# A decoder layer on one core: whole-row loads of p, first products by halves of depth, other banks for the first stacks, y split in four portions

## The chip, the cores and the metric

The kernel runs on one core of a Trainium2 chip. The metric is the device time of one execution in microseconds (us): before the change the median of three runs is 2273.17 us (2273.09 to 2273.24). Engines: TensorE (PE; PEld is its weight load), VectorE (DVE), ScalarE (ACT), GpSimd (POOL) and SyncE (SP), whose queue issues the loads and stores. Each engine works its instructions in order.

## The reference

One hybrid decoder layer on 1024 tokens of width 1024, all in float32:

```python
x = x + 0.5 * swiglu(rms_norm(x, ffn1_norm), ffn1_w_gate, ffn1_w_up, ffn1_w_down)      # d_ff 2816
h = rms_norm(x, mix_norm)
fq, fk, fv, f_logit, sq, sk, sv, g_fox, g_sb = split_columns(h @ w_in)
y_fox = forgetting_attention(rms_norm(fq, q_norm), rms_norm(fk, k_norm), fv, log_sigmoid(f_logit + forget_bias))
y_sb = stick_breaking_attention(sq, sk, sv)                                            # 8 heads of 64 each
x = x + (sigmoid(g_fox) * (y_fox @ w_branch_fox) + sigmoid(g_sb) * (y_sb @ w_branch_sb)) @ w_out
x = x + 0.5 * swiglu(rms_norm(x, ffn2_norm), ffn2_w_gate, ffn2_w_up, ffn2_w_down)
x = x + sigmoid(rms_norm(x, ple_norm) @ w_ple_gate) * (p @ w_ple_proj)                 # p: 1024 x 256
```

## The kernel before

A product of float32 operands is made of three: each operand is split into a high part (rounded, a CAST on ACT, line 112 or 136) and a low part (the rest, a subtraction on DVE, line 113, or on POOL, line 146), and high x high, low x high and high x low are added in one PSUM bank. There are eight banks: three `sc`, two `pt`, one `av`, two `pf`; `ps2` goes round the `sc` and `av` banks, `ps1` round `pt` and `pf`. A bank is used again only when its readers are through.

**The start** (`first_entry`). x is not needed for the last term's product p @ w_ple_proj, so the kernel makes it first and stores it (`pd`). p comes transposed, 256 x 1024; p and its weights are each two blocks k of 128 rows and 1024 columns. Eight loads of half blocks (`load_p`: block k, columns half h) are issued by SP, six of them ahead of the tiles of x. `busy(10)` gives TensorE ten matmuls on zeros meanwhile. `project(t, d)` makes the product of token tile t and half d of the width: six matmuls (line 1208), three products by two blocks k. Between the 16 calls stand the norms of the first four x tiles: `norm_stat` (ACT, POOL), `norm_mul` (DVE), and the transposes `norm_high` (TensorE, line 219, then ACT) and `norm_low` (DVE). The first products of the feed-forward follow (`plain`, line 419) with transposes of the other four tiles in `combo_a`. In this part the order of each engine's work is as the code is written.

**Attention**. There a scheduler orders instructions by itself within the given dependencies. `forget_sums` is followed by a gate unit and the first stacks: `fox_stack_units` transposes normalized q and k (line 785) into a `pf` bank, and `fill_stacks` reads it with two ACT and two DVE instructions (lines 770 to 773). Units of projections (`nat_steps`, line 691, `feat_steps`, line 699), each in a `pf` bank, are interleaved as filling with 16 heads of four steps c: `scores` (lines 889, 890; reductions at 894, exp at 900, its scaling on POOL at 902; the stick-breaking scans at 865) and `apply` (transposes 941, their parts 943 on ACT and 944 on DVE, values 963).

**y**. From head 14 on, the finished outputs y of the attention come back from memory: `load_y` loads blocks of 128 rows, `split_y` splits each (one ACT and one DVE instruction of 128 x 1024). `Y_AT` says at which head and step: first what is split, then what is loaded. Blocks 4 to 6 go into the buffer of blocks 0 to 2.

Of the kernel before, what the change touches and what calls it, by code (L numbers as in the profile page):

```python
# [18 lines left out]
P = 128  # L19
S = 1024  # L20
D = 1024
# [17 lines left out]
def tile_hybrid_decoder_layer(  # L39
# [33 lines left out]
    def bank(tag):  # L73
        return pp.tile([P, 512], F32, tag=tag, bufs=PSUM[tag], name=nm("ps"))
# [5 lines left out]
    def ps2():  # L80
        ring[1] += 1
        return bank(("sc", "sc", "sc", "av")[ring[1] % 4])
# [4 lines left out]
    def pe(ins):  # L87
        order("pe", ins)
# [99 lines left out]
    def busy(n):  # L188

        if "zero" not in last:  # L190
            last["zero"] = slot("T", [P, 512], BF16)
            nc.vector.memset(last["zero"][:], 0.0)
        z, ps = last["zero"], bank("av")
        for _ in range(n):
            pe(nc.tensor.matmul(ps[:], z[:, 0:P], z[:], start=True, stop=True))
# [17 lines left out]
    def norm_mul(N, t):  # L213
        nc.vector.scalar_tensor_tensor(N["h"][t][:], N["x"][:, t, :], N["r"].pop(t)[:], N["g"][:], ALU.mult, ALU.mult)
# [559 lines left out]
        nc.sync.dma_start(f(KH[a, cs]), f(KH[b, cs]))  # L774
        nc.sync.dma_start(f(KL[a, cs]), f(KL[b, cs]))

    def fox_stack_units(cell, hh, out_cell):
        def unit(half):
            if half == 0:
                out_cell["st"] = new_stacks()  # L780
            cs = slice(half * 512, half * 512 + 512)
            N = cell["n"][half]
            ps = bank("pf")
            for q in range(4):
                pe(nc.tensor.transpose(ps[:, q * P:(q + 1) * P], N[:, q, hh].rearrange("p s d -> p (s d)"), identf[:]))
# [238 lines left out]
    def attention():  # L1024
# [160 lines left out]
    def first_entry(F):  # L1185

        def load_x(t):
            nc.sync.dma_start(X[t // 4][:, t % 4, :], x[0, t * P:(t + 1) * P, :])

        raw = {"p": [slot("T", [P, S]) for _ in range(2)], "w": [slot("Q", [P, D]) for _ in range(2)]}  # L1190
        src = {"p": kp(p), "w": kp(w_ple_proj[0])}
        op = {"p": slot("H", [P, 2, 2, S], F32R), "w": slot("H", [P, 2, 2, D], F32R)}
        outs = {}

        def load_p(a, k, h):
            cs = slice(h * 512, h * 512 + 512)
            nc.sync.dma_start(raw[a][k][:, cs], src[a][:, k, cs])

        def split_p(a, k, h, eng_lo):
            cs = slice(h * 512, h * 512 + 512)  # L1200
            split(op[a][:, 0, k, cs], op[a][:, 1, k, cs], raw[a][k][:, cs], nc.scalar, eng_lo)

        def project(t, d):
            ps = ps2()
            i = 0
            for a, b in ((0, 0), (1, 0), (0, 1)):
                for k in range(2):
                    pe(nc.tensor.matmul(ps[:], op["p"][:, a, k, t * P:(t + 1) * P], op["w"][:, b, k, d * 512:d * 512 + 512], start=(i == 0), stop=(i == 5)))  # L1208
                    i += 1
            if d == 0:  # L1210
                outs[t] = slot(("RAW", "RAW", "GF", "RN", "Q", "Q")[t % 6], [P, D])
                nc.scalar.copy(outs[t][:, 0:512], ps[:])
            else:
                nc.vector.tensor_copy(outs[t][:, 512:D], ps[:])
# [5 lines left out]
        def projects(t):  # L1220
            project(t, 0)
            project(t, 1)

        for h, a in ((0, "pw"), (1, "w")):
            for k in range(2):
                for c in a:
                    load_p(c, k, h)
# [10 lines left out]
        for k in range(2):  # L1238
# [6 lines left out]
        load_x(4)  # L1245
        store_p(0)
        norm_stat(N[0], 0, "PT", True)
        projects(1)
        norm_mul(N[0], 0)
        load_x(5)  # L1250
        store_p(1)
        norm_stat(N[0], 1, "WL", True)
        projects(2)
        norm_mul(N[0], 1)
        for k in range(2):
            split_p("p", k, 1, nc.gpsimd)
        load_x(6)
        store_p(2)
        norm_stat(N[0], 2, "WL", True)
        projects(3)  # L1260
        norm_mul(N[0], 2)
        load_x(7)
        store_p(3)
        norm_stat(N[0], 3, "PT", True)
        norm_high(N[0], 0, ps1)
        projects(4)
        norm_low(N[0], 0)
        norm_mul(N[0], 3)
        F["load"](1)
        store_p(4)  # L1270
        norm_high(N[0], 1, ps1)
        projects(5)
        norm_low(N[0], 1)
        store_p(5)
        norm_high(N[0], 2, ps1)
        F["prep"](0, 1)
        projects(6)
        norm_low(N[0], 2)
        store_p(6)
        norm_high(N[0], 3, ps1)  # L1280
        norm_stat(N[1], 0, "Y", True)
        projects(7)
        norm_low(N[0], 3)
        store_p(7)
        F["prep"](0, 2)
        norm_stat(N[1], 1, "Y", True)
        F["plain"](0, 0, (0,))
        norm_mul(N[1], 0)
        norm_stat(N[1], 2, "PT", True)
        norm_mul(N[1], 1)  # L1290
# [263 lines left out]
```

## Time and profile before

| | |
|---|---|
| median of three runs | 2273.17 us |
| profiled execution | 2273.31 us, its span 2271.6 us |
| TensorE busy | 2247.5 us |
| granted clock, mean | 0.997 |
| DVE, ACT, POOL busy | 1467.7, 975.5, 821.8 us |

The span runs from the first to the last instruction. In a timeline or wait row the bracket names how long the engine was idle before and what ended that. Rows by windows give busy time of PE, PEld, DVE, ACT and POOL, then the granted TensorE clock, the share of the DMA engines and GB/s. "DMA to landing" is the time from issue to the end of a transfer.

### The profile page before, as it was taken

How to read it: one execution, taken by the hardware profiler on the slowest of the kernel's cores; microseconds unless marked ns; L12 is line 12 of the kernel's file. 1: busy time of each engine (PE TensorE's matmuls, PEld its weight loads, DVE VectorE, ACT ScalarE, POOL GpSimd, SP SyncE). 2: the span in 40 equal slices, each digit the busy share in tenths (PEclk: the TensorE clock that was granted, in tenths of full speed). 3: DMA queues.
4: the chain of work that ended last, by engine and by line, in shares of the span. 5: the costliest groups of instructions: out<-in, count | busy, mean ns of one | idle time of the engine just before them, and what ended most of it. 6: DMA issues, size and time to landing. Idle time of an engine off the chain costs nothing.

```text
span 2271.6 us, 30620 instructions
## 1 busy us (share of the span) xinstructions
PE 2247.5 (99%) x11440; PEld 1911.8 (84%) x11440; DVE 1467.7 (65%) x2206; ACT 975.5 (43%) x1740; POOL 821.8 (36%) x756
## 2 busy tenths in 40 slices
PE   8999999999999999999999999999999999999999
PEld 6888888888889999998988888888888888888887
DVE  6955555487874566656666676889655555778752
ACT  6433333333343455555555564246333333434431
POOL 1144343410024546645556644410534343200111
PEclk9999999999999999999999999999999999999999
DMA  6223232474431222222124245832423232656132
GB/s 250 70 101 127 79 130 79 156 288 148 158 131 48 84 75 71 75 66 72 50 70 116 61 125 196 287 121 65 139 79 130 79 130 79 252 195 217 64 103 92
DMA packets 186949, 276.01 MB, mean 122 GB/s; under 512 B 27176, under 2 KB 109352, under 8 KB 186800
## 3 DMA queue, kind: packets, MB, share of 16 engines
q1 hardware_dynamic: 186800, 274.05, 36.2%
q8 instruction: 90, 1.47, 0.3%
q14 instruction: 59, 0.48, 0.1%
HBM read 190.35 MB, written 75.27 MB: 117 GB/s over the span
## 4 chain that ended last, share of the span: by engine, by line
PE 95%; DVE 3%; ACT 1%; issue 1%; DMA 0%; POOL 0%; SPq 0%; POOLq 0%; DVEq 0%; ACTq 0%
PE ps L464 35%; PE ps L359 21%; PE ps L699 11%; PE ps L691 8%; PE ps L1496 4%; PE ps L1159 4%; PE ps L963 3%; PE ps L941 3%; PE ps L890 1%; PE ps L889 1%; PE ps L419 1%; PE ps L1208 1%; PE ps L219 1%; DVE RN L865 1%; DVE H L113 0%
## 5 line engine op out<-in xcount | busy, mean ns | idle before, releaser
L359 PE MATMUL ps<-H,H 128*128 128x512 f32 x2184 | 497.7, 389 | 1.2 <-DVE X L367 1.2
L359 PEld LDWEIGHTS ps<-H,H 128*128 128x128 f32 x2184 | 409.3, 188 | 86.7 <-issue 2.0
L464 PE MATMUL ps<-H,WL 128*128 128x512 f32 x1008 | 239.4, 389 | 0.8 <-ACT WL L112 0.8
L464 PEld LDWEIGHTS ps<-H,WL 128*128 128x128 f32 x1008 | 189.1, 188 | 40.5 <-ACT WL L112 1.2
L699 PE MATMUL ps<-H,WH 128*128 128x512 f32 x768 | 210.4, 401 | 1.4 <-DVE PT L814 1.4
L699 PEld LDWEIGHTS ps<-H,WH 128*128 128x128 f32 x768 | 136.2, 188 | 24.4 <-DVE PT L814 2.1
L146 POOL TENSOR_TENSOR WL<-Y,WH 128x512 fp32r<-128x512 f32 (+1 forms) x10 | 14.4, 1467 | 382.6 <-ACT WH L136 382.6
L944 DVE TENSOR_TENSOR PT<-ps,PT 128x512 fp32r<-128x512 f32 (+1 forms) x160 | 101.1, 633 | 75.4 <-ACT PT L943 74.5
L146 POOL TENSOR_TENSOR WL<-RAW,WH 128x512 fp32r<-128x512 f32 (+1 forms) x104 | 124.1, 1214 | 61.0 <-ACT WH L136 47.8
L464 PE MATMUL ps<-H,Q 128*128 128x512 f32 x600 | 143.1, 389 | 0.0
L367 DVE SCALAR_TENSOR_TENSOR X<-ps,X 128x512 f32<-128x512 f32 x168 | 109.0, 687 | 50.9 <-PE ps L359 50.9
L691 PE MATMUL ps<-WH,H 128*128 128x256 f32 (+1 forms) x896 | 133.6, 288 | 3.7 <-DVE KL L773 2.1
L464 PEld LDWEIGHTS ps<-H,Q 128*128 128x128 f32 x600 | 112.6, 188 | 23.4
L943 ACT CAST PT<-ps 128x512 fp32r<-128x512 f32 (+1 forms) x160 | 87.4, 548 | 95.4 <-PE ps L941 94.0
L691 PEld LDWEIGHTS ps<-WH,H 128*128 128x128 f32 x896 | 117.8, 191 | 5.6 <-issue 2.3
L464 PE MATMUL ps<-X,WL 128*128 128x512 f32 x504 | 121.1, 389 | 0.0
L464 PEld LDWEIGHTS ps<-X,WL 128*128 128x128 f32 x504 | 94.6, 188 | 19.6
L699 PE MATMUL ps<-H,WL 128*128 128x512 f32 x384 | 108.5, 399 | 0.0
L963 PE MATMUL ps<-PT,X 128*128 128x256 f32 (+1 forms) x640 | 103.9, 282 | 3.9 <-DVE PT L944 3.9
L963 PEld LDWEIGHTS ps<-PT,X 128*128 128x128 f32 x640 | 94.2, 190 | 15.2 <-DVE PT L944 6.0
L902 POOL TENSOR_TENSOR T<-T,l 128x128 f32<-128x128 f32 (+3 forms) x64 | 73.3, 1149 | 93.0 <-DVE l L901 90.6
L260 POOL TENSOR_TENSOR PT<-GF,RN 128x512 f32<-128x512 f32 x20 | 33.2, 1658 | 186.0 <-DVE GF L507 101.8
(400 smaller groups left out, 4725.4 us busy)
## 6 DMA issues: line engine op xcount, KB each, us to landing
hidden<-PT SPq DMA_DIRECT2D x40, 512.0 KB, 3.0
WH<-in_ffn_w_gate_dram SPq DMA_DIRECT2D x38, 512.0 KB, 4.8
Q<-hidden SPq DMA_DIRECT2D x24, 512.0 KB, 6.6
hidden<-RN SPq DMA_DIRECT2D x22, 512.0 KB, 2.6
RAW<-in_w_in_dram SPq DMA_DIRECT2D x22, 512.0 KB, 4.4
KH<-in_ffn_w_up_dram SPq DMA_DIRECT2D x20, 512.0 KB, 6.2
KL<-in_ffn_w_up_dram SPq DMA_DIRECT2D x20, 512.0 KB, 6.9
T<-in_ffn_w_down_dram SPq DMA_DIRECT2D x20, 512.0 KB, 4.8
```

What stands on the lines that cost most here:

```text
L146: ins = eng_lo.tensor_sub(lo[part], raw[part], f(hi[part]))
L359: pe(nc.tensor.matmul(groups[g][t][:], act[:, a, k, t * P:(t + 1) * P], wt[:, b, k, :], start=(fresh and n == 0), stop=(i in (6, 1, 4) and ...
L367: nc.vector.scalar_tensor_tensor(xs, groups[g][t][:], scale, xs, ALU.mult, ALU.add)
L464: pe(nc.tensor.matmul(ps[:], hl[:, a, k, :], rhs(m, b, k), start=(first and i == 0), stop=(final and i == 11), skip_group_check=True))
L691: pe(nc.tensor.matmul(ps[:, :n], hT[t // 4][a][:, k, (t % 4) * P:(t % 4 + 1) * P], w[k // 4][b][:, k % 4, :n], start=(i == 0), stop=(i == ...
L699: pe(nc.tensor.matmul(ps[:], w[a][:, k, :], hT[half][b][:, k, :], start=(i == 0), stop=(i == 23)))
L902: nc.gpsimd.tensor_mul(T[:, :n], T[:, :n], l[:].broadcast_to([P, n]))
L943: high = nc.scalar.copy(pt[:, 0, :width], ps[:, :width])
L944: low = nc.vector.tensor_sub(pt[:, 1, :width], ps[:, :width], f(pt[:, 0, :width]))
L963: pe(nc.tensor.matmul(o, lh, r, start=(kpair == c and i == 0), stop=(kpair == 0 and i == 3)))
L1159: pe(nc.tensor.matmul(ps[:], w[a][:, k, :], yT[g][b][:, k, half * 512:half * 512 + 512], start=(i == 0), stop=(i == 11)))
L1496: pe(nc.tensor.matmul(ps, hT[t // 4][a][:, k, (t % 4) * P:(t % 4 + 1) * P], pl["w"][d, k // 2][b][:, k % 2, cs], start=(i == 0), stop=(i = ...
```

## The change

Three edits. (1) At the start p and its weights come in four loads of whole blocks; eleven dummy matmuls instead of ten; `project` takes several units and goes through the blocks k outermost, so that the first call works at four banks, all products of block 0 ahead of those of block 1; the eviction alternates between ACT and DVE by t + d; two x tiles are loaded ahead of the gain and all others behind, and norms, `prep` and `combo_a` are placed anew. (2) The first stacks (h = 0) use the `pt` banks. (3) The splits of y stand in four places instead of two.

```diff
-        def load_p(a, k, h):
-            cs = slice(h * 512, h * 512 + 512)
-            nc.sync.dma_start(raw[a][k][:, cs], src[a][:, k, cs])
+        def load_p(a, k):
+            nc.sync.dma_start(raw[a][k][:], src[a][:, k, :])
...
-        def project(t, d):
+        def project(units, ring):
+            banks = [ring() for _ in units]
             i = 0
-            for a, b in ((0, 0), (1, 0), (0, 1)):
-                for k in range(2):
+            for k in range(2):
+                for a, b in ((0, 0), (1, 0), (0, 1)):
+                    for ps, (t, d) in zip(banks, units):
+                        pe(nc.tensor.matmul(ps[:], op["p"][:, a, k, t * P:(t + 1) * P], op["w"][:, b, k, d * 512:d * 512 + 512], start=(i == 0), stop=(i == 5)))
                     i += 1
+            for ps, (t, d) in zip(banks, units):
+                if t not in outs:
+                    outs[t] = slot(("RAW", "RAW", "GF", "RN", "Q", "Q", "T", "T")[t], [P, D])
+                if (t + d) % 2:
+                    nc.vector.tensor_copy(outs[t][:, d * 512:d * 512 + 512], ps[:])
+                else:
+                    nc.scalar.copy(outs[t][:, d * 512:d * 512 + 512], ps[:])
...
+        for k in range(2):
+            for c in "pw":
+                load_p(c, k)
         nc.scalar.activation(stat([P, 1], "ss")[:], mhalf[:, 0:1], AF.Silu)
-        busy(10)
+        busy(11)
         for k in range(2):
             for c in "pw":
                 split_p(c, k, 0, nc.vector)
         load_x(0)
+        load_x(1)
         N.append(combo_begin(X[0], ffn1_norm[0]))
         N.append(combo_begin(X[1], None, N[0]))
-        for t in range(1, 4):
+        for t in range(2, NT):
             load_x(t)
-        for k in range(2):
-            load_p("p", k, 1)
         F["load"](0)
-        project(0, 0)
+        project([(t, 0) for t in range(4)], ps2)
         for k in range(2):
             split_p("w", k, 1, nc.vector)
-        project(0, 1)
...
         norm_stat(N[0], 0, "PT", True)
...
         for k in range(2):
             split_p("p", k, 1, nc.gpsimd)
+        norm_stat(N[0], 1, "WL", True)
+        project([(0, 1)], ps1)
+        norm_mul(N[0], 0)
+        project([(1, 1)], ps1)
...
+        norm_high(N[0], 0, ps1)
+        project([(4, 0)], ps2)
+        norm_low(N[0], 0)
+        norm_mul(N[0], 2)
+        project([(4, 1)], ps2)
...
         F["plain"](0, 0, (0,))
         norm_mul(N[1], 1)
+        norm_stat(N[1], 3, "PT", True)
         F["prep"](0, 5)
-        norm_stat(N[1], 3, "PT", True)
+        F["a"](0)
+        norm_mul(N[1], 2)
         F["plain"](0, 0, (1,), False)
-        norm_mul(N[1], 2)
-        F["a"](0)
+        F["a"](1)
         norm_mul(N[1], 3)
-        F["a"](1)
...
-            ps = bank("pf")
+            ps = bank(tag)
...
-            return fox_stack_units(qk[h // 2], h % 2, stacks[h])
+            return fox_stack_units(qk[h // 2], h % 2, stacks[h], "pt" if h == 0 else "pf")
...
-    Y_AT = {(14, 0): ((), range(4)), (14, 3): (range(4), (4, 5, 6)), (15, 1): ((4, 5, 6), ())}
+    Y_AT = {(14, 0): ((), range(4)), (14, 3): ((0, 1), ()), (15, 0): ((2, 3), (4, 5, 6)), (15, 1): ((4, 5), ()), (15, 2): ((6,), ())}
```

What it makes of the engines' rows is shown at three places (a number behind a name tells the buffers apart). First TensorE at the start, before and after, from the last dummy on; H_102 holds p, H_103 the weights:

```order
L195 MATMUL ps_114<-T_112 128x512
L1208 MATMUL ps_147<-H_103,H_102 128x512 x6
L1208 MATMUL ps_160<-H_103,H_102 128x512 x6
L1208 MATMUL ps_176<-H_103,H_102 128x512 x6
L1208 MATMUL ps_185<-H_103,H_102 128x512 x6
```

```order
L195 MATMUL ps_112<-T_110 128x512
L1208 MATMUL ps_148<-H_103,H_102 128x512
L1208 MATMUL ps_149<-H_103,H_102 128x512
L1208 MATMUL ps_150<-H_103,H_102 128x512
L1208 MATMUL ps_151<-H_103,H_102 128x512
```

Six matmuls in a row went to one bank; now they go round four banks, and that six times, before single banks follow. ACT at the same place, before and after, from the last of the first four casts:

```order
L112 CAST H_103<-Q_101 128x512
L1212 COPY RAW_154<-ps_147 128x512
L112 CAST H_103<-Q_100 128x512
L112 CAST H_103<-Q_101 128x512
L206 ACTIVATE PT_170,ss_171<-X_94 128x1024
```

```order
L112 CAST H_103<-Q_101 128x512
L1216 COPY RAW_176<-ps_148 128x512
L1216 COPY GF_180<-ps_150 128x512
L112 CAST H_103<-Q_100 128x512
L112 CAST H_103<-Q_101 128x512
L206 ACTIVATE PT_188,ss_189<-X_94 128x1024
```

Two copies out of banks now stand ahead of the casts of the weights' other halves.

Second, DVE behind the first stacks (T and l belong to the first step's score tiles), from the fill of the second half of the first stack, before and after:

```order
L772 SCALAR_TENSOR_TENSOR Q_5684<-ps_5726,gqk,Q_5684 64x512
L773 SCALAR_TENSOR_TENSOR KL_5686<-ps_5726,gqk,KH_5685 64x512
L901 RECIPROCAL l_5744<-l_5744 128x1
L772 SCALAR_TENSOR_TENSOR Q_5753<-ps_5756,gqk,Q_5753 64x512
L773 SCALAR_TENSOR_TENSOR KL_5755<-ps_5756,gqk,KH_5754 64x512
L894 ISA T_5808,m_5809<-GF_5737,ps_5812 128x128
```

```order
L772 SCALAR_TENSOR_TENSOR Q_5681<-ps_5723,gqk,Q_5681 64x512
L773 SCALAR_TENSOR_TENSOR KL_5683<-ps_5723,gqk,KH_5682 64x512
L901 RECIPROCAL l_5741<-l_5741 128x1
L894 ISA T_5805,m_5806<-GF_5734,ps_5809 128x128
L894 ISA m_5806 128x1
L772 SCALAR_TENSOR_TENSOR Q_5750<-ps_5753,gqk,Q_5750 64x512
L773 SCALAR_TENSOR_TENSOR KL_5752<-ps_5753,gqk,KH_5751 64x512
```

The first reduction of the second score tile (T_5808, now T_5805) has moved ahead of the fill of the next stack. Third, DVE at (14,3); H<-X are the splits of y, before and after:

```order
L865 SCALAR_TENSOR_TENSOR RN_12369<-GF_12368,RN_12369 128x384
L113 TENSOR_TENSOR H_12439<-X_12127,H_12438 128x1024 x3
L983 TENSOR_TENSOR Y_12126<-ps_12386,Y_12126 64x256
L113 TENSOR_TENSOR H_12439<-X_12127,H_12438 128x1024
L865 SCALAR_TENSOR_TENSOR RN_12453<-GF_12452,mask_sb 128x128
```

```order
L865 SCALAR_TENSOR_TENSOR RN_12366<-GF_12365,RN_12366 128x384
L113 TENSOR_TENSOR H_12436<-X_12124,H_12435 128x1024 x2
L983 TENSOR_TENSOR Y_12123<-ps_12383,Y_12123 64x256
L865 SCALAR_TENSOR_TENSOR RN_12443<-GF_12442,mask_sb 128x128
L865 SCALAR_TENSOR_TENSOR RN_12443<-GF_12442,RN_12443 128x383
```

Of four splits two stay. The other two are found at the change from (14,3) to (15,0), here in the changed kernel:

```order
L944 TENSOR_TENSOR PT_12533<-ps_12528,PT_12533 128x512
L983 TENSOR_TENSOR Y_12123<-ps_12492,Y_12123 64x256
L113 TENSOR_TENSOR H_12436<-X_12124,H_12435 128x1024 x2
L865 SCALAR_TENSOR_TENSOR RN_12568<-GF_12567,mask_sb 128x127
L944 TENSOR_TENSOR PT_12603<-ps_12599,PT_12603 128x384
```

They follow the end of (14,3)'s values (L983) and stand ahead of the first scan and the first low part (L944) of (15,0).

More of the change, by code (lines that the diff above doesn't have):

```diff
@@ L775, in fill_stacks, with fox_stack_units @@
         nc.sync.dma_start(f(KL[a, cs]), f(KL[b, cs]))
-    def fox_stack_units(cell, hh, out_cell):
+    def fox_stack_units(cell, hh, out_cell, tag="pf"):
         def unit(half):
@@ L1218, in store_p @@
                 nc.sync.dma_start(pd[t * P:(t + 1) * P, :], outs[t][:])
[L1220 to L1224, printed above, removed]
-            for k in range(2):
-                for c in a:
-                    load_p(c, k, h)
+        for k in range(2):
+            for c in "pw":
+                load_p(c, k)
         nc.scalar.activation(stat([P, 1], "ss")[:], mhalf[:, 0:1], AF.Silu)
-        busy(10)
+        busy(11)
         for k in range(2):
@@ L1233, in first_entry @@
         load_x(0)
+        load_x(1)
         N.append(combo_begin(X[0], ffn1_norm[0]))
         N.append(combo_begin(X[1], None, N[0]))
-        for t in range(1, 4):
+        for t in range(2, NT):
             load_x(t)
-        for k in range(2):
-            load_p("p", k, 1)
         F["load"](0)
-        project(0, 0)
+        project([(t, 0) for t in range(4)], ps2)
         for k in range(2):
             split_p("w", k, 1, nc.vector)
-        project(0, 1)
-        load_x(4)
-        store_p(0)
@@ L1261, in first_entry @@
-        norm_mul(N[0], 2)
[L1262 to L1269, printed above, removed]
+        store_p(0, 1)
+        project([(2, 1)], ps1)
+        norm_mul(N[0], 1)
+        project([(3, 1)], ps1)
+        norm_stat(N[0], 3, "PT", True)
+        store_p(2, 3)
+        F["load"](1)
+        norm_high(N[0], 0, ps1)
+        project([(4, 0)], ps2)
@@ L1270, in first_entry @@
+        norm_low(N[0], 0)
+        norm_mul(N[0], 2)
+        project([(4, 1)], ps2)
         store_p(4)
         norm_high(N[0], 1, ps1)
-        projects(5)
+        project([(5, 0)], ps2)
         norm_low(N[0], 1)
+        norm_mul(N[0], 3)
+        project([(5, 1)], ps2)
         store_p(5)
+        norm_stat(N[1], 0, "Y", True)
         norm_high(N[0], 2, ps1)
+        project([(6, 0)], ps2)
+        norm_low(N[0], 2)
         F["prep"](0, 1)
-        projects(6)
-        norm_low(N[0], 2)
+        project([(6, 1)], ps2)
@@ L1279, in first_entry @@
         store_p(6)
+        norm_stat(N[1], 1, "Y", True)
         norm_high(N[0], 3, ps1)
-        norm_stat(N[1], 0, "Y", True)
-        projects(7)
+        project([(7, 0)], ps2)
         norm_low(N[0], 3)
+        F["prep"](0, 2)
+        project([(7, 1)], ps2)
         store_p(7)
-        F["prep"](0, 2)
-        norm_stat(N[1], 1, "Y", True)
-        F["plain"](0, 0, (0,))
         norm_mul(N[1], 0)
         norm_stat(N[1], 2, "PT", True)
+        F["plain"](0, 0, (0,))
         norm_mul(N[1], 1)
+        norm_stat(N[1], 3, "PT", True)
```

17 lines of the change are left out of this document (removed).

## The prediction

> **What bounds it now.** I read the page first, then TensorE's waits, the timeline of the first 45 us, the clock by windows, and the timelines around the waits.
>
> ```profile
> PE 2247.5 (99%) x11440; PEld 1911.8 (84%) x11440; DVE 1467.7 (65%) x2206; ACT 975.5 (43%) x1740; POOL 821.8 (36%) x756
> PE ps L1208 <- ACT H L112: 4.1, 3, 2.5
> PE ps L963 <- DVE PT L944: 3.9, 5, 1.6
> PE ps L691 <- DVE KL L773: 2.1, 1, 2.1
> ```
>
> TensorE is busy 2247.5 of 2271.6 us: the kernel is its matmuls, and the change takes none of those away. It can only win back idle time (24.1 us in all; the waits above, "total, times, longest", and some smaller ones below are the ones in reach) and time at a low clock. The clock is the second bound:
>
> ```profile
> 7.00:8.00 1.00, 0.00 (x0) 0.00 (x0) 0.51 (x1) 0.21 (x1) 0.00 (x0) 0.85 0.88 291
> 8.00:9.00 1.00, 0.54 (x1) 0.50 (x2) 0.56 (x1) 0.41 (x1) 0.00 (x0) 0.50 1.07 432
> 17.00:18.00 1.00, 1.00 (x4) 0.71 (x4) 0.00 (x0) 0.23 (x1) 0.00 (x0) 0.53 1.11 353
> 751.00:752.00 1.00, 1.00 (x10) 1.00 (x10) 0.98 (x2) 0.00 (x0) 0.03 (x1) 0.90 0.78 156
> 754.00:757.00 3.00, 3.00 (x21) 2.90 (x20) 1.63 (x9) 1.36 (x4) 0.66 (x2) 0.80 0.43 87
> 1384.00:1387.00 3.00, 1.43 (x11) 1.07 (x10) 2.48 (x4) 0.99 (x2) 2.21 (x3) 1.00 0.96 250
> 1387.00:1390.00 3.00, 3.00 (x19) 2.56 (x18) 1.67 (x3) 1.07 (x2) 0.45 (x1) 1.00 0.86 319
> ```
>
> (Third number from the right: granted clock.) It halves at 7.70 (0.85 = 0.70 full + 0.30 half) and returns at 17.94 (0.53): 10.24 us. It halves again at 751.9 and returns at 755.2. 10.24 is three times 3.41, and 3.4 us is the second stretch, so I read the gate as deciding every 3.41 us, in the first stretch at 7.70, 11.11, 14.53 and 17.94.
>
> ```profile
> 1.27 3.81 PE L195 MATMUL ps<-T 128*128 128x512 bf16 x10 [1.27 <-DVE T L192]
> 5.50 0.49 PE L1208 MATMUL ps<-H,H 128*128 128x512 f32 x1 [0.42 <-ACT H L112]
> 8.46 2.50 PE L1208 MATMUL ps<-H,H 128*128 128x512 f32 x5 [2.47 <-ACT H L112]
> 50.54 3.02 PE L419 MATMUL ps<-H,WH 128*128 128x512 f32 x12 [0.48 <-ACT WH L112]
> 77.02 5.76 PE L464 MATMUL ps<-H,WL 128*128 128x512 f32 x24 [0.79 <-ACT WL L112]
> 12.15 12.59 PE ps L1208 x42
> 25.61 2.75 PE ps L1208 x12
> ```
>
> The last two rows are of the chain. From 4.29 to 7.70 TensorE worked about 1.2 of 3.41 us: the clock fell. From 7.70 to 11.11 it worked 2.5 us, to 14.53 2.4 us: it stayed low. Only the full interval to 17.94 raised it. At full clock a product costs 2.75 / 12 = 0.229 us, at half about 0.45. The 48th product ends at 12.15 + 12.59 = 24.74; that is my mark.
>
> **The start.** Six loads of half rows (256 KB each) become four of whole rows (512 KB).
>
> ```profile
> 1.23 0.42 SPq L1197 DMA_DIRECT2D Q<-in_w_ple_proj_dram  x1
> 4.83 0.62 ACT L112 CAST H<-Q 128x512 fp32r<-128x512 f32 x1 [0.36 <-DMA Q<-in_w_ple_proj_dram]
> 7.79 0.62 ACT L112 CAST H<-Q 128x512 fp32r<-128x512 f32 x1 [1.01 <-DMA Q<-in_w_ple_proj_dram]
> L1188 SPq DMA_DIRECT2D X<-in_x_dram x1: 432/432/432, 3.6 to 3.6; - x1
> DMA to landing us min/median/max: 6.8/6.8/6.8
> 11.00 0.59 ACT L1212 COPY RAW<-ps 128x512 f32<-128x512 f32 x1 [2.59 <-PE ps L1208]
> 11.48 1.14 ACT L112 CAST H<-Q 128x512 fp32r<-128x512 f32 x2
> ```
>
> ACT's waits end at the landings: two half loads (0.52 MB) by 4.83, four (1.05 MB) by 7.79; the load of the first whole X tile, which closes 2.10 MB, by 3.6 + 6.8 = 10.4. So the first megabyte comes at about 180 GB/s, the second at 400. Nothing shows a whole-row load as the first one, so I bound it: the changed kernel's second load completes 1.05 MB, at 5.3 (400 GB/s from 2.0 on, and 0.7 to land) to 7.8 (the row). I take 7.1, nearer the slow end, which is the same bytes in the same place. The fourth, 2.10 MB, is then there by about 10.
>
> First product: 7.1 + 0.67 (from 4.83 to 5.50 in the rows) = 7.77. The clock falls at 7.70, since the interval from 4.29 holds only the tail of the eleven dummy matmuls (to 5.3, 1.0 us). But the first half of depth now has twelve products for four banks, 5.4 us at half clock, and the second half (cast by 10.7, low part 0.7 later) is ready before they end. So TensorE works 7.77 to 11.11 without a gap, 98% of the interval, and the clock rises at 11.11, not 17.94. Products: 3.34 / 0.45 = 7.4 by then, the other 16.6 at 0.229 take 3.8: 24 done at 14.9. Then comes the old stall in new form: ACT must copy out two banks (0.59 each) before it casts the weights' other halves; the row pair 11.00, 11.48 cost 1.19 us before. Here two copies, partly under the last products, then a cast 0.62, then DVE's low part 0.69: 1.2 + 0.3 = 1.5. Twenty-four more products take 5.5: the 48th ends at 21.9, against 24.74: **2.8 won** (ends: 0.8 and 5.1, worked out in the rivals). The eleventh dummy runs in idle time: nothing.
>
> What this must not uncover: all x tiles are issued ahead of the gate weights now, and at 400 GB/s their last lands near 22, some 10 us ahead of its use; copies, norms and POOL's low parts of p's second half stand 0.6 to 1 us ahead of their users in the count. Whole-row stores of the last two outputs from T instead of RAW must land before DVE writes T again; about 1 us of room. Behind it, the first transposes of the second half now come before the second half of the gate product, 2.7 us earlier in TensorE's order, so the ACT and DVE chain behind the waits of 0.48 and 0.79 starts earlier: of those 1.27 I take **0.8** (0 to 1.27).
>
> **The first stacks.** With two pf banks, the stack's second half held one until its four readers were through.
>
> ```profile
> 741.22 3.92 PE L699 MATMUL ps<-H,WH 128*128 128x512 f32 x16 [0.35 <-DVE PT L814]
> 747.75 0.66 PE L785 MATMUL ps<-identf,RN 128*128 128x128 f32 x4 [0.17 <-DVE PT L814]
> 750.07 0.68 ACT L771 ACTIVATE KH<-ps,gqk 64x512 fp32r<-64x512 f32 x1
> 750.51 0.95 PE L691 MATMUL ps<-WH,H 128*128 128x256 f32 x6 [2.10 <-DVE KL L773]
> 751.54 0.76 DVE L773 SCALAR_TENSOR_TENSOR KL<-ps,gqk,KH 64x512 fp32r<-64x512 f32 x1
> 754.70 0.61 POOL L902 TENSOR_TENSOR T<-T,l 128x256 f32<-128x256 f32 x1 [3.67 <-DVE l L901]
> 757.10 0.49 PE L941 MATMUL ps<-identf,T 128*128 128x128 f32 x3
> ```
>
> On pt the first two stacks free both pf banks: 0.35 + 0.17 + 2.10 of waits go, and with them the 3.4 us at half clock (1.7 us): 4.3. Part comes back. The first q/k unit then ends at about 751.2 (24 products of 0.109 and the scores between), and its successor needs the bank of the next stack, whose fill still runs ACT, ACT, DVE, DVE and now stands behind one more reduction on DVE: free at 752.1 instead of 752.3. New wait 0.8. Then the transposes L941 need POOL's product of row 754.70, which the DVE chain gives by 754.3: another 1.1. They end 2.8 before 757.6; a last 0.3 goes at the next values. **2.6 won** (0.9 if the two new waits lower the clock again, 4.3 if neither comes).
>
> **The splits of y.**
>
> ```profile
> 1326.21 2.95 ACT L112 CAST H<-X 128x1024 fp32r<-128x1024 f32 x3
> 1327.99 4.29 DVE L113 TENSOR_TENSOR H<-X,H 128x1024 fp32r<-128x1024 f32 x3
> 1332.08 0.50 PE L889 MATMUL ps<-KH,Q 128*128 128x512 f32 x1 [0.58 <-ACT T L898]
> 1338.92 0.50 PE L963 MATMUL ps<-PT,X 128*128 128x128 f32 x2 [1.23 <-DVE PT L944]
> 1343.41 0.62 PE L963 MATMUL ps<-PT,X 128*128 128x256 f32 x3 [0.63 <-DVE PT L944]
> 1347.97 0.56 DVE L944 TENSOR_TENSOR PT<-ps,PT 128x384 fp32r<-128x384 f32 x1 [2.16 <-ACT PT L943]
> 1350.19 0.62 PE L963 MATMUL ps<-PT,X 128*128 128x256 f32 x4
> ```
>
> All four stood at (14,3): 4 x 1.05 on ACT, 4.29 and one more on DVE, and three waits follow. Two go to (15,0): DVE is 2.6 us earlier, more than the longest wait, so 0.58 + 1.23 + 0.63 = 2.4 go. At (15,0) the two cost ACT 2.1 and DVE 2.4, ahead of L944: it ends near 1349.4 instead of 1348.5, under the 1350.19 at which TensorE uses it. The load of y's block 6 now waits for the split of block 2 at (15,0), two portions ahead of its use. The wait of 1.57 at 1385.9 follows the scans of (15,3), whose work is unchanged: it stays. **2.4 won** (1 to 2.5: below, if TensorE, now earlier too, catches DVE at (15,0)).
>
> **Sum.** 2.8 + 0.8 + 2.6 + 2.4 = 8.6. The profiled execution took 2273.31 (span 2271.6 and 1.7 around it), 0.14 above the median: 2264.7.
>
> **Rivals.**
> *The clock holds.* If the second load is there by 6.0, products start at 6.7, the interval to 7.70 is worked 2.0 of 3.41 us, and the clock need not fall: idle time of 1.57 in the row of 1384 left it at 1.00 there and in the next. Twelve products end at 9.4, the other twelve follow the fourth load to 12.6, the 48th at 19.6: 5.1, total 2262.4. For it: 400 GB/s once X loads; against: the first megabyte's 180. The Trainium skill, "TensorE: Matmul & The Clock Gate", section "Why this matters for your kernels", says that gaps up to about 3 us do not lower the clock; by that rule this rival holds for any landing here. The trace disagrees: a gap of 2.10 lowered it.
> *The first product is late.* At a landing of 7.8 it starts at 8.45, the interval to 11.11 is worked 78%, between the 73% that did not raise the clock and the whole one that did; if it does not, the clock rises at 14.53: 13.4 products by then, 24 at 16.95, the 48th at 23.95: 0.8, total 2266.7. The Trainium skill, "DMA: Bandwidth & Descriptors", section "Specifications", has rows of 512 B at line rate already, so that longer rows bring nothing and this rival holds. The trace agrees in part: among the loads that end by 10.4 at 400 GB/s two have half rows.
> *The new waits lower the clock.* 0.8 and 1.1 in one interval of 3.41: 1.7 back, 2266.4. The gap rows put the edge between 1.57 and 2.10, so it needs both whole.
> *Slower.* The clock stays at half through the projections, since waits for the loads and the stall of 1.5 break up every interval. Start at 8.45: the first part breaks even if the clock rises at about 17.7, each further us costs half a us, so the 5.8 of the other parts is gone at 29, and at 38, near the end of the projections, it stands at 2277.7. Against it: one whole interval of work raised the clock at 17.94, and the first twelve products at half clock already fill one.
>
> **Chances.** Forecast 0.50 (2263.5 to 2266), clock holds 0.20, first product late 0.15, new waits 0.10, slower 0.02, something unseen 0.03. What a measurement tells from no change is about 0.2%, 4.5 us: "within" needs two of the bad cases at once: 0.06; slower 0.03; faster 0.91. The range reaches from the clock that holds with full gains elsewhere, 2260.8, to late product and new waits together, 2268.6.
>
> **What would show it.** Right: half clock once, near 7.7 to 11.1; TensorE unbroken after the first product but for one stall near 15; no wait of 2 us and clock 1.00 near 745; no L889 or L963 wait from 1315 to 1340. Wrong: a first product after 8.2, half clock beyond 11.2, a wait before the transposes of the second half, or L963 waits at (15,0).

## The result, and the profile after

The median is 2262.69 us (five runs, 2262.15 to 2262.73) against 2273.17 (2273.07 to 2273.26): 10.5 us less, ratio 0.9953, interval 0.9939 to 0.9968. The forecast was 2264.7 (2260.8 to 2268.6). The profiled execution of the changed kernel took 2262.69, its span 2261.0.

TensorE's busy time from the page, 4.3 us less than before, and from the list of its waits the one at the start (total, times, longest); idle time fell from 24.1 to 17.8 us. So of 10.6 us of span 6.3 are idle time and 4.3 busy time: mostly matmuls that no longer run at half clock, less the 0.8 us by which the dummies now take longer.

```profile
PE 2243.2 (99%) x11441; PEld 1907.6 (84%) x11441; DVE 1468.5 (65%) x2206; ACT 975.4 (43%) x1740; POOL 820.2 (36%) x756
PE ps L1208 <- ACT H L112: 1.8, 3, 1.0
```

The timeline of the start, TensorE and then two of ACT's casts, and the clock in the two slices with the most idle time:

```profile
1.27 4.62 PE L195 MATMUL ps<-T 128*128 128x512 bf16 x11 [1.27 <-DVE T L192]
6.41 3.02 PE L1208 MATMUL ps<-H,H 128*128 128x512 f32 x12 [0.51 <-ACT H L112]
9.69 3.01 PE L1208 MATMUL ps<-H,H 128*128 128x512 f32 x12 [0.27 <-ACT H L112]
13.71 6.02 PE L1208 MATMUL ps<-H,H 128*128 128x512 f32 x24 [1.00 <-ACT H L112]
...
5.74 0.62 ACT L112 CAST H<-Q 128x512 fp32r<-128x512 f32 x1 [0.64 <-DMA Q<-in_w_ple_proj_dram]
9.02 0.62 ACT L112 CAST H<-Q 128x512 fp32r<-128x512 f32 x1 [0.63 <-DMA Q<-in_w_ple_proj_dram]
...
6.00:7.00 1.00, 0.59 (x3) 0.51 (x4) 0.61 (x1) 0.35 (x1) 0.00 (x0) 1.00 1.00 410
13.00:14.00 1.00, 0.29 (x1) 0.29 (x2) 0.89 (x2) 1.00 (x3) 0.00 (x0) 1.00 1.05 426
```

The second load is there at 5.74, the first product starts at 6.41, and the granted clock (third number from the right) is 1.00 in every slice from 4 to 20. The 48th product ends at 13.71 + 6.02 = 19.73 instead of 24.74. What the DMA engines moved from 4 to 5 (last number, GB/s), before and after:

```profile
4.00:5.00 1.00, 1.00 (x5) 0.23 (x2) 0.50 (x1) 0.64 (x2) 0.00 (x0) 1.00 0.77 285
...
4.00:5.00 1.00, 1.00 (x4) 0.30 (x2) 0.00 (x0) 0.52 (x1) 0.00 (x0) 1.00 1.02 393
```

The first stacks: TensorE's two waits there, and the clock around them; before, it was 0.68 from 750 to 755.

```profile
746.45 1.31 PE L691 MATMUL ps<-WH,H 128*128 128x256 f32 x9 [0.63 <-DVE KL L773]
748.33 0.44 PE L941 MATMUL ps<-identf,T 128*128 128x128 f32 x2 [0.46 <-POOL T L902]
...
745.00:750.00 5.00, 3.91 (x30) 3.27 (x29) 4.04 (x17) 3.03 (x9) 2.11 (x4) 1.00 0.81 201
750.00:755.00 5.00, 5.00 (x42) 5.00 (x41) 3.47 (x15) 1.94 (x5) 1.37 (x3) 1.00 0.00 0
```

The values behind (14,3): TensorE's waits, and what DVE does ahead of the second one.

```profile
1330.38 0.62 PE L963 MATMUL ps<-PT,X 128*128 128x256 f32 x3 [0.35 <-DVE PT L944]
1332.90 0.62 PE L963 MATMUL ps<-PT,X 128*128 128x256 f32 x3 [0.64 <-DVE PT L944]
...
1325.78 0.68 DVE L767 TENSOR_TENSOR Q<-ps,Q 64x512 fp32r<-64x512 f32 x1 [0.82 <-ACT KH L766]
...
1330.24 2.02 DVE L865 TENSOR_TENSOR_SCAN RN<-GF,RN 128x512 f32<-128x512 f32 x1
1332.18 0.66 DVE L944 TENSOR_TENSOR PT<-ps,PT 128x512 fp32r<-128x512 f32 x1
```

The waits of 0.58 and 1.23 are gone. The one of 0.63 is still there, as 0.64, and one of 0.35 is new.

Four waits that both kernels have serve as marks, first in the kernel before, then in the changed one. They cut the span into the start, the stretch with the first stacks, attention, and the stretch with the splits of y.

```profile
600.19 2.06 PE L359 MATMUL ps<-H,H 128*128 128x512 f32 x8 [0.62 <-DVE X L367]
812.83 0.63 PE L691 MATMUL ps<-WH,H 128*128 128x256 f32 x3 [0.49 <-DVE X L113]
1256.49 0.62 PE L963 MATMUL ps<-PT,X 128*128 128x256 f32 x3 [0.23 <-DVE PT L944]
2095.92 4.33 PE L359 MATMUL ps<-H,H 128*128 128x512 f32 x18 [0.62 <-DVE X L367]
```

```profile
594.67 7.50 PE L359 MATMUL ps<-H,H 128*128 128x512 f32 x32 [0.62 <-DVE X L367]
803.98 0.63 PE L691 MATMUL ps<-WH,H 128*128 128x256 f32 x3 [0.48 <-DVE X L113]
1247.55 0.62 PE L963 MATMUL ps<-PT,X 128*128 128x256 f32 x3 [0.23 <-DVE PT L944]
2085.53 14.75 PE L359 MATMUL ps<-H,H 128*128 128x512 f32 x64 [0.61 <-DVE X L367]
```

| stretch | before | after | won |
|---|---|---|---|
| to the first mark | 600.19 | 594.67 | 5.52 |
| first to second (first stacks) | 212.64 | 209.31 | 3.33 |
| second to third | 443.66 | 443.57 | 0.09 |
| third to fourth (splits of y) | 839.43 | 837.98 | 1.45 |

The sum is 10.39; another 0.2 lies behind the last mark.

### The profile page after: what moved, and what is told of

It reads as the page before. It is cut to its first block, busy times and chain, and to the rows that moved or that the text cites. A ratio compares the mean times of both kernels' runs of the same rounds, so it can differ in the third digit from the quotient of the medians.

```text
span 2261.0 us, 30610 instructions
## 1 busy us (share of the span) xinstructions
PE 2243.2 (99%) x11441; PEld 1907.6 (84%) x11441; DVE 1468.5 (65%) x2206; ACT 975.4 (43%) x1740; POOL 820.2 (36%) x756
## 4 chain that ended last, share of the span: by engine, by line
PE 95%; DVE 3%; ACT 1%; issue 1%; DMA 0%; POOL 0%; SPq 0%; POOLq 0%; DVEq 0%; ACTq 0%
PE ps L464 35%; PE ps L359 21%; PE ps L699 11%; PE ps L691 7%; PE ps L1490 4%; PE ps L1159 4%; PE ps L963 3%; PE ps L941 3%; PE ps L419 1%; PE ps L890 1%; PE ps L889 1%; PE ps L219 1%; PE ps L1208 1%; DVE RN L865 1%; DVE H L113 0%
## 5 line engine op out<-in xcount | busy, mean ns | idle before, releaser
L944 DVE TENSOR_TENSOR PT<-ps,PT 128x512 fp32r<-128x512 f32 (+1 forms) x160 | 101.1, 633 | 73.0 <-ACT PT L943 71.8
L464 PEld LDWEIGHTS ps<-X,WL 128*128 128x128 f32 x504 | 94.6, 188 | 19.6
L963 PE MATMUL ps<-PT,X 128*128 128x256 f32 (+1 forms) x640 | 104.1, 282 | 3.1 <-DVE PT L944 3.1
L963 PEld LDWEIGHTS ps<-PT,X 128*128 128x128 f32 x640 | 94.2, 190 | 14.6 <-DVE PT L944 5.3
```

What stands on the lines that cost most here:

```text
L464: pe(nc.tensor.matmul(ps[:], hl[:, a, k, :], rhs(m, b, k), start=(first and i == 0), stop=(final and i == 11), skip_group_check=True))
L944: low = nc.vector.tensor_sub(pt[:, 1, :width], ps[:, :width], f(pt[:, 0, :width]))
L963: pe(nc.tensor.matmul(o, lh, r, start=(kpair == c and i == 0), stop=(kpair == 0 and i == 3)))
```

## The experiments

Executions of the kernel before differed by up to 2.3 us on one chip here (27 runs, 2271.74 to 2274.05) and by more on another (15 runs, 2268.55 to 2273.70). Their mean granted clock differs too, from 0.997 to 0.999. The edits elsewhere are therefore read from the stretches between the marks; times are given beside them.

**The banks alone.** The kernel before with the second edit only.

```diff
-            ps = bank("pf")
+            ps = bank(tag)
...
-            return fox_stack_units(qk[h // 2], h % 2, stacks[h])
+            return fox_stack_units(qk[h // 2], h % 2, stacks[h], "pt" if h == 0 else "pf")
```

> The kernel before with the first stacks on the pt banks and nothing else. Theory (what the traces of before and after show at their marks): the waits of 0.35, 0.17 and 2.10 and the 3.4 us at half clock go, new waits of about 0.6 and 0.5 come: 3.3 us less, 2269.9 us, clock 1.00 from 745 to 760. Rival 1: the gain leans on the start (the gate's intervals fall otherwise when TensorE comes 5.5 us later), the clock falls once near 750 even so: 1.6 less, 2271.6. Rival 2, the recorded term of 2.6 with waits of 0.8 and 1.1: 2270.6.

Measured: 2269.52 us (11 runs, 2268.82 to 2270.61) beside 2272.92, ratio 0.9986 (0.9977 to 0.9994). Its wait, the clock there, and its first two marks:

```profile
750.99 1.30 PE L691 MATMUL ps<-WH,H 128*128 128x256 f32 x9 [0.63 <-DVE KL L773]
750.00:755.00 5.00, 3.90 (x30) 3.34 (x29) 3.82 (x17) 3.01 (x9) 2.56 (x5) 1.00 0.78 193
...
599.17 3.19 PE L359 MATMUL ps<-H,H 128*128 128x512 f32 x13 [0.61 <-DVE X L367]
808.53 0.62 PE L691 MATMUL ps<-WH,H 128*128 128x256 f32 x3 [0.48 <-DVE X L113]
```

The stretch takes 808.53 - 599.17 = 209.36, 3.28 less than before and as much as in the full change, with the same wait of 0.63 and the clock at 1.00. So the gain does not need the changed start (rival 1, as far as one trace can say), and 2.6 was too small (rival 2).

**The splits of y alone.** The kernel before with the third edit only.

```diff
-    Y_AT = {(14, 0): ((), range(4)), (14, 3): (range(4), (4, 5, 6)), (15, 1): ((4, 5, 6), ())}
+    Y_AT = {(14, 0): ((), range(4)), (14, 3): ((0, 1), ()), (15, 0): ((2, 3), (4, 5, 6)), (15, 1): ((4, 5), ()), (15, 2): ((6,), ())}
```

> The kernel before with the splits of y in four places and nothing else. Theory: the waits of 0.58 and 1.23 before the values of (14,3) go, the one of 0.63 stays because scans of 2.0 us stand ahead of L944 on DVE, and one of 0.35 is new: 1.4 us less, 2271.7 us. Rival (the recorded term): all three go when TensorE is not also earlier by the other edits: 2.4 less, 2270.8.

Measured: 2270.77 us (11 runs, 2270.06 to 2272.09), ratio 0.9992 (0.9983 to 1.0001): the median lies at the rival's 2270.8, but the times don't tell the edit from no change, let alone 1.4 from 2.4. The profiled execution, the longest of the eleven (2272.09), does by its waits and last two marks:

```profile
1339.48 0.61 PE L963 MATMUL ps<-PT,X 128*128 128x256 f32 x3 [0.34 <-DVE PT L944]
1341.99 0.62 PE L963 MATMUL ps<-PT,X 128*128 128x256 f32 x3 [0.64 <-DVE PT L944]
...
1256.69 0.62 PE L963 MATMUL ps<-PT,X 128*128 128x256 f32 x3 [0.23 <-DVE PT L944]
2094.67 5.71 PE L359 MATMUL ps<-H,H 128*128 128x512 f32 x24 [0.62 <-DVE X L367]
```

The stretch takes 837.98, 1.45 less, with the same two waits as in the full change, although no other edit makes TensorE earlier here.

**No split at (14,3).** The changed kernel with all four at (15,0).

```diff
-(14, 3): ((0, 1), ()), (15, 0): ((2, 3), (4, 5, 6))
+(15, 0): (range(4), (4, 5, 6))
```

> The changed kernel with no split of y at (14,3): all four at (15,0). Theory: the waits of 0.35 and 0.64 before the values of (14,3) stand (DVE's scans make them, not the splits), and DVE at (15,0) has 2.4 us more ahead of its first low part, which leaves TensorE waiting there about 1 us: 2263.7. Rival (the two splits left at (14,3) make those waits): they go, 1.0 less, and unless (15,0) costs something 2261.7.

Measured: 2263.34 us (2263.10 to 2264.21). Its stretch between the third and fourth mark takes 838.66, 0.7 more than in the changed kernel. Two of its three waits there:

```profile
1332.50 0.62 PE L963 MATMUL ps<-PT,X 128*128 128x256 f32 x3 [0.61 <-DVE PT L944]
1340.17 0.50 PE L963 MATMUL ps<-PT,X 128*128 128x128 f32 x2 [0.55 <-DVE PT L944]
```

Without any split there, the wait of 0.64 is 0.61 (and that of 0.35 is 0.21); the one of 0.55 at (15,0) is new. The splits don't make the remaining waits: the low part L944 stands behind a scan of 2.02 on DVE, and that scan behind a queue that begins when ACT delivers KH (row 1325.78).

**More dummies in the kernel before.**

```diff
-        busy(10)
+        busy(17)
```

> The kernel before with 17 dummy matmuls instead of ten, nothing else: TensorE works on zeros from 1.3 to about 8.4, where the second product's operands are there. Theory (the start's gain is mostly the clock that holds): no half clock before 18; the first six products end near 9.9 instead of 11.0, the next start at 11.1 instead of 12.15, the 48th ends near 21.6 instead of 24.74: 3.1 less, 2270.1 us. Rival (the gain is the order of the products and the loads): the clock falls anyway or does not matter, 2273.2, within 0.5.

Measured: 2269.89 us (11 runs, 2269.19 to 2272.68), ratio 0.9989 (0.9981 to 0.9998). In the profiled execution the 48th product ends at 22.63, 2.1 earlier, and the clock does fall, once. TensorE, and the slices in which the clock falls and returns:

```profile
6.35 0.58 PE L1208 MATMUL ps<-H,H 128*128 128x512 f32 x1
8.40 1.45 PE L1208 MATMUL ps<-H,H 128*128 128x512 f32 x5 [1.47 <-ACT H L112]
11.04 11.59 PE L1208 MATMUL ps<-H,H 128*128 128x512 f32 x42 [1.19 <-ACT H L112]
...
11.00:12.00 1.00, 0.96 (x2) 0.63 (x3) 0.98 (x2) 1.00 (x2) 0.00 (x0) 0.67 1.00 406
14.00:15.00 1.00, 1.00 (x5) 0.76 (x4) 0.69 (x1) 0.00 (x0) 0.00 (x0) 0.62 1.00 389
```

The theory's time came, but the trace shows less of its mechanism: half clock for 3.4 us instead of 10.2, where I expected none. This execution is not the median's. It took 2271.04 and is one of five with a mean clock of 0.998 (2270.76 to 2272.68); the other six, with 0.999, took 2269.19 to 2269.89. The half clock near 750, which this kernel keeps (3.4 us), makes 0.999 by itself, so in those six the clock of the start seems to have held, as the theory has it; none of them has a trace. In this one, 0.67 is full for 0.34 us: it fell at 11.34; 0.62 is half for 0.76: it returned at 14.76. The interval that ended at 11.34 was worked from 8.40 to 9.85 and from 11.04, about 1.75 of 3.41 us. No wait was longer than 1.5 us; parts of two came together.

**Fewer dummies in the changed kernel.**

```diff
-        busy(11)
+        busy(6)
```

> The changed kernel with six dummy matmuls instead of eleven: they end near 3.8, and the first product still starts at 6.4. Theory (the gate sums the work in fixed intervals of 3.41 us): the interval from 4.29 to 7.70 then holds only 1.3 us of work, the clock falls at 7.70 and returns at 11.11; 24 products end at 14.2 instead of 12.07: 2.1 more than the changed kernel, 2264.8 us. Rival (only a gap of about 3 us or more lowers the clock; this one is 2.6): clock 1.00 throughout, 2262.7.

Measured: 2264.27 us (2263.67 to 2264.99), ratio to the kernel before 0.9963 (0.9950 to 0.9975). TensorE's first products, and the clock:

```profile
6.34 7.38 PE L1208 MATMUL ps<-H,H 128*128 128x512 f32 x24 [2.33 <-ACT H L112]
...
7.00:8.00 1.00, 1.00 (x5) 0.78 (x4) 0.02 (x1) 0.00 (x0) 0.00 (x0) 0.84 0.98 340
11.00:12.00 1.00, 1.00 (x6) 0.82 (x5) 0.00 (x0) 0.00 (x0) 0.00 (x0) 0.96 1.04 352
```

The clock fell at 7.68 after a gap of 2.33 us and returned at 11.08. The 24th product ended at 13.72, a little less late than expected.

**One bank after another.** The changed kernel with the first four products in turn.

```diff
-        project([(t, 0) for t in range(4)], ps2)
+        for t in range(4):
+            project([(t, 0)], ps2)
```

> The changed kernel with the first four products one after the other (each with both halves of depth before the next bank begins); whole-row loads and all else as in the changed kernel. Theory (the order over four banks fills the wait for the second half of depth and so holds the clock): three products from 6.4, then nothing until 9.7, so the interval to 11.1 is worked about 40% and the clock falls there until 14.5; 24 products end near 16.7 instead of 12.7, part of that is won back because the copies out of banks no longer come all at once: 3.0 more than the changed kernel, 2265.7 us. Rival (whole rows make the gain, the order does little): the clock stays at 1.00, 24 products end 2.0 later at most and the stall behind them is gone: 2263.7 or less.

Measured: 2266.22 us (11 runs, 2263.92 to 2267.24); the changed kernel took 2262.57 on the same chip (below). TensorE behind the second half of depth, and the clock:

```profile
9.34 7.50 PE L1208 MATMUL ps<-H,H 128*128 128x512 f32 x23 [1.56 <-ACT H L112]
...
10.00:11.00 1.00, 1.00 (x4) 0.80 (x4) 0.01 (x1) 0.39 (x1) 0.00 (x0) 0.72 0.83 340
13.00:14.00 1.00, 1.00 (x4) 0.81 (x3) 0.69 (x1) 0.00 (x0) 0.00 (x0) 0.57 1.06 434
```

3.65 us more, in the profiled execution with half clock from 10.44 to 13.86. Its first mark is 3.2 later than the changed kernel's: 1.7 of that is the half clock, 1.3 the wait of 1.56 where there was one of 0.27. One of the eleven executions has a mean clock of 1.000, the others 0.998 or 0.999; it took 2263.92, 1.35 more than the changed kernel, about what that wait alone costs. Whole rows without the order over four banks hold neither the clock nor most of the gain.

**Half-row loads in the changed kernel.**

```diff
-        def load_p(a, k):
-            nc.sync.dma_start(raw[a][k][:], src[a][:, k, :])
+        def load_p(a, k, h):
+            cs = slice(h * 512, h * 512 + 512)
+            nc.sync.dma_start(raw[a][k][:, cs], src[a][:, k, cs])
...
-        for k in range(2):
-            for c in "pw":
-                load_p(c, k)
+        for h, a in ((0, "pw"), (1, "w")):
+            for k in range(2):
+                for c in a:
+                    load_p(c, k, h)
...
         load_x(0)
         load_x(1)
...
+        for k in range(2):
+            load_p("p", k, 1)
```

> The changed kernel with half-row loads in the old order of loads (p and w of block 0, of block 1, left halves; then the right halves of w, then x, p's right halves behind two x tiles); order of the products, banks and all else as in the changed kernel. Theory (halves of depth over four banks make the gain, row length does not): the first two loads are there by 4.8, the first product follows the last dummy at about 5.9, the next half of depth is there by 7.8, no gap, 24 products end at about 12.0, clock 1.00: 2262.7 us, within 0.5. Rival (whole rows make the gain): second load and first product as late as with whole rows or the second half of depth late, half clock from 7.70: 2264.7 or more.

Measured: 2261.86 us (2261.79 to 2262.20), ratio to the kernel before 0.9952 (0.9939 to 0.9966). Its products (one line further down in this file):

```profile
6.09 5.73 PE L1209 MATMUL ps<-H,H 128*128 128x512 f32 x24 [0.84 <-ACT H L112]
12.83 6.00 PE L1209 MATMUL ps<-H,H 128*128 128x512 f32 x24 [1.00 <-ACT H L112]
```

All 24 without a gap, the 48th at 18.83, 0.9 earlier than with whole rows. The time is 0.8 less than expected. The long rows are not what brings the gain; they cost a little, since a product needs the left halves alone, and those complete sooner by themselves: the casts of p's and the weights' second blocks start at 6.28 and 7.77 here, at 7.77 and 9.02 with whole rows.

**Casts ahead of the copies.** The changed kernel; `split_p("w", k, 1)` is called between the first products and their four copies.

```diff
-        def project(units, ring):
+        def project(units, ring, between=None):
...
+            if between is not None:
+                between()
             for ps, (t, d) in zip(banks, units):
                 if t not in outs:
...
-        project([(t, 0) for t in range(4)], ps2)
-        for k in range(2):
-            split_p("w", k, 1, nc.vector)
+        project([(t, 0) for t in range(4)], ps2, lambda: [split_p("w", k, 1, nc.vector) for k in range(2)])
```

> The changed kernel with the splits of the weights' right halves ahead of the four copies out of banks, so that ACT need not copy first; nothing else. Theory (the stall of 1.4 us after the 24th product is ACT's order): casts run before 12.0, the stall goes, 1.2 less than the changed kernel, 2261.5 us. Rival: the right halves' products then wait for something else (DVE's low parts behind it, or the copies that come later hold the banks at 18): 2262.3 or more.

Measured: 2261.27 us (2260.99 to 2261.35). ACT's casts and TensorE's products:

```profile
8.73 1.66 ACT L112 CAST H<-Q 128x512 fp32r<-128x512 f32 x3 [0.65 <-DMA Q<-in_w_ple_proj_dram]
...
6.50 11.46 PE L1208 MATMUL ps<-H,H 128*128 128x512 f32 x48 [0.36 <-ACT H L112]
```

48 products without a gap, the last ends at 17.96. So the stall was the order in which casts and copies stand. The edit moves DVE's low parts with ACT's casts; what TensorE waited for in the changed kernel was ACT's cast (row 13.71).

**Both.** The last two edits together, run twice, the second time beside the changed kernel itself.

> Both: half-row loads in the old order and the splits of the weights' right halves ahead of the copies. Theory: 24 products unbroken from 5.9 to 12.0, the next ones at once, the 48th ends near 18.2 instead of 19.7: 1.4 less than the changed kernel, 2261.3 us. Rival (the loads of the right halves are behind with half rows, or p's right halves come late for the tiles 4 to 7): a wait for them, 2262.3 or more.

> The version with half-row loads and the splits of the weights' right halves ahead of the copies, on the same chip as the changed kernel: 2.2 us less than that, 2260.4 us, since the 48th product ends 2.4 earlier in its trace. Rival (the difference between the two was one of chips): within 0.5 of the changed kernel.

> The changed kernel once more, on the same chip as the kernels beside it: 2262.7 us, within 0.5; clock 1.00 from 4 to 20 and from 740 to 760.

Measured: 2260.41 us (2260.07 to 2261.57), and 2260.18 (2260.03 to 2260.72) where the changed kernel took 2262.57 (2262.45 to 2263.18). Its products in the second run:

```profile
5.16 3.02 PE L1209 MATMUL ps<-H,H 128*128 128x512 f32 x12
8.51 8.46 PE L1209 MATMUL ps<-H,H 128*128 128x512 f32 x36 [0.33 <-ACT H L112]
```

The 48th ends at 16.97. This version is 2.4 us faster than the changed kernel on one chip, without an overlap of the runs; against the kernel before its ratio is 0.9950 (0.9938 to 0.9962).

**Both, with six dummies.** `busy(6)` instead of `busy(11)` in that version.

> The version with half-row loads and the splits of the weights' right halves ahead of the copies, with six dummy matmuls instead of eleven: they end at 4.0, the first product starts at 5.6. Theory (the gate goes by the share of an interval of 3.41 us that is worked, and the edge lies between 42% and 54%): the interval from 4.3 to 7.7 holds 2.1 us of work, 62%, so the clock holds: 2260.4 us, within 0.5. Rival (any gap of more than 1.57 us lowers it, here 1.6, or the dummies must reach the first product): half clock from 7.7 to 11.1, 1.5 more, 2261.9.

Measured: 2261.76 us (2261.01 to 2263.18). The theory's 2260.4 was missed. The median is the rival's time (2261.9), but the trace, of the longest of the five executions, doesn't show its mechanism. Its products, and TensorE and clock in two slices:

```profile
6.16 13.89 PE L1209 MATMUL ps<-H,H 128*128 128x512 f32 x48 [2.15 <-ACT H L112]
...
10.00:11.00 1.00, 1.00 (x3) 0.74 (x3) 0.00 (x0) 0.00 (x0) 0.00 (x0) 1.00 0.87 338
13.00:14.00 1.00, 1.00 (x7) 0.79 (x6) 0.00 (x0) 0.04 (x1) 0.00 (x0) 1.00 1.05 428
```

The granted clock shows no fall, but 48 products took 13.89 us instead of 11.5: three or four at work in a slice until 12, six or seven from then on. Until then they ran at the rate of the first dummies (six in 2.74 us). I read this as a low state from the start that is left only near 12, and that the column of the granted clock doesn't show. Two things agree. With 17 dummies, four of them are at work in a slice from 2 to 4 and six from 5 to 6, at a granted clock of 1.00 in both. And of the five executions of the changed kernel with six dummies, the three with a mean clock of 1.000 took longer (2264.27 to 2264.99) than the two with 0.999 (2263.67 and 2263.82). No run tests it by itself.

## Why the prediction was right, and where its steps were off

The sign and the range held; the time was 2.0 us below the forecast, at that of the rival "the clock holds" (2262.4). The forecast's own mechanism at the start, half clock from 7.70 to 11.11, did not come; the range held because its lower end allowed for that rival. That the total meets the rival's so closely is partly luck: the other three terms, taken at 5.8, brought about 5.3, since 0.7 too little at the first stacks and nearly 1.0 too much at the splits of y almost cancel. Of the four signs of being right one came in full, the clock of 1.00 near 745 without a wait of 2 us; the clock did not halve at the start, the stall there came at 13 and not near 15, and two L963 waits stayed between 1315 and 1340. None of the signs of being wrong came. By its steps:

- **The start (2.8 forecast, 5.0 measured at the 48th product).** The step that failed is the time of the second load: 7.1 taken, 5.74 measured. I chose the slow end, since half rows had brought the same megabyte by 7.79; the fast end (5.3) was nearer. The 180 GB/s behind that choice is a misreading: by the windows of the kernel before, 1.09 MB had moved by 6.0 and about 1.65 by 7.79, at 233 to 332 GB/s in each us, so loads behind the fourth were under way too. In the changed kernel 1.05 MB had moved by 5.0. So the first product started at 6.41 instead of 7.77; the dummies, too, ended later than taken, at 5.89 and not 5.3, and no interval was idle enough. The rival's numbers came out one by one: load 6.0 and 5.74, start 6.7 and 6.41, 48th product 19.6 and 19.73, won 5.1 and 5.0. Runs show where it comes from: with one bank after another the start wins 2.3 (first mark at 597.89), so the order over four banks brings 3.2 of the 5.5; with half rows it wins 6.4 (593.77). What brings the other 2.3 (the copies on two engines, the new places of the norms, the eleventh dummy) was not taken apart. The stall behind the 24th product came, but as 1.00 instead of 1.5 (last of the four banks done at 12.7, next product 13.71), and it was the order of casts and copies.
- **The gate's times.** I read 7.70, 11.11 and so on as times at which any execution decides. The spacing is right, the times are not: see the last section. The fall read as 751.9 is at 751.8 (0.90 is half for 0.2 us). Nor is there an edge between gaps of 1.57 and 2.10: one of 1.56 lowered the clock with one bank after another. Of the two rules weighed, that of the Trainium skill ("TensorE: Matmul & The Clock Gate", section "Why this matters for your kernels", gaps up to about 3 us do no harm) is contradicted again, by gaps of 2.33 and of twice less than 1.5. The other ("DMA: Bandwidth & Descriptors", section "Specifications", rows of 512 B at line rate) would have had the load at 7.8; the trace disagrees, 5.74, but two loads also stand in place of four, and no run separates the length of a row from the number of loads.
- **The chain behind 0.48 and 0.79 (0.8 forecast, 0.5).** The first wait went, the second stayed at 0.78. TensorE came 5.0 earlier and the chain as much.
- **The first stacks (2.6 forecast, 3.3).** The mechanism was right, the new waits too large: 0.63 and 0.46 for 0.8 and 1.1, and the "last 0.3" did not show. (The working gives 2.4 or 2.5, not 2.6: 4.3 less 0.8 and 1.1, or 2.8 less 0.3.) The rival "new waits lower the clock" fell: 1.00 in both kernels with this edit.
- **The splits of y (2.4 forecast, 1.45).** The step "DVE is 2.6 us earlier, so 0.58 + 1.23 + 0.63 go" failed for the third wait: its L944 starts at 1332.18, where it started at 1342.70: 10.52 earlier, 8.94 of that by the edits ahead, so 1.58 by this one, and TensorE, rid of 1.81 of waits, came earlier by more. It is held by scans that follow ACT's KH; with the splits taken out altogether they hold it just so. The reason kept for the low end, TensorE early by the other edits, was not it.
- **Nothing uncovered.** Whole-row stores from T and the x tiles made no new wait. The prediction's count of six half loads is short: eight are replaced, two of them issued behind x tiles; no term rests on them.

The "first product late" and "slower" rivals did not occur: the clock held.

## What to carry to other kernels

Where several outputs wait for two halves of an operand, work all banks on the first half before any goes on to the second: here that filled the wait which a single output left open, and kept the clock. Ahead of an engine's in-order queue, put what the next matmuls need before what only frees buffers. A move of work off an engine wins a wait only if that engine's queue from its last own wait on is shorter for it: look for the idle time on that engine between the work moved and the instruction waited for.

## What the runs showed of the hardware

The gate's intervals are 3.41 us long (10.24 us of half clock are three of them), and within one execution they go on unchanged: in the kernel before the clock fell at 7.70 and at 751.8, 744.1 us apart, which is 218 intervals; with the splits of y alone at 7.98 and 752.1, again 218; with 17 dummies at 11.34 and 748.6, 216. Where they begin differs between executions. Three kernels have the same start: the clock fell at 7.70 in the kernel before, at 7.98 with the splits of y alone and at 10.24 with the banks alone. It fell at 7.68 with six dummies, at 10.44 with one bank after another and at 11.34 with 17 dummies, and each time it returned after one or several such intervals. The Trainium skill says so too ("TensorE: Matmul & The Clock Gate", Part 1: the window runs freely and the cold stretch varies with its phase at the start); the traces agree.

Kernels with a broken start vary accordingly, as I take it: 3.3 us between eleven executions for one bank after another, 2.3 for the kernel before on the chip with 27 runs, against 0.4 to 0.7 in five runs each for the changed kernel and for half rows, in whose starts no interval of 3.41 us can be idle for more than about 1.0. No run sets the phase, so this is not shown, and it isn't the whole: the five first runs of both edits together, with 48 products unbroken, lie 1.5 apart.

What share of an interval keeps the clock stays open. With about half it fell (17 dummies; one bank after another, 1.85 us worked from 7.03 to 10.44, 54%). But the wait of 1.56 to 1.58 that all 14 traces have between 1371 and 1386 left it at 1.00 in all of them. If the intervals go on as above, that wait lay whole inside one in the kernel before (1384.37 to 1385.94, the interval from 1383.3 to 1386.7), which was then worked 54% as well. So neither the length of a gap nor the share of busy time, in which the ends of matmuls are modelled, tells the two apart.
